# One prompt tile's gate matrix by scattered adds in DRAM, and row gathers paced anew

## The chip, the cores and the metric

One core of a Trainium2 chip runs the whole program. The metric is device time in microseconds (us) from the start to the end of an execution of the program; the profiled execution has its own time, given below beside the runs'. The engines are called as in the profile: PE (TensorE, matrix products), DVE (VectorE), ACT (ScalarE), POOL (GpSimd) and SP (SyncE, which only issues DMAs here). Each takes its instructions in a fixed order that was set when the program was built. DMAs are issued by SP, ACT and POOL.

## What is computed

An encoder layer is applied to two batches with shared weights: a prompt of 512 tokens and a sample of 256, of 1024 features. After attention and an output projection comes PEER, a layer of 128 x 128 = 16384 single-neuron experts:

```
q   = (xc @ w_q)                                  # 8 heads, two halves of 128
sc  = einsum('cpzk,znk->cpzn', q, sub_keys)       # scores of 128 keys for each half
top_v, top_i = top_k(sc, 16)
cand = top_v[:, :, 0, :, None] + top_v[:, :, 1, None, :]
best, pos = top_k(cand, 16)                       # 16 experts for each head and token
eidx = take_along_axis(cand_idx, pos)             # i * 128 + j
g   = softmax(best)
act = gelu(einsum('cd,cpkd->cpk', xc, u[eidx]))
out = einsum('cpk,cpkd->cd', g * act, v[eidx])    # 8 x 16 = 128 experts for each token
```

So each token weighs 128 of 16384 experts. All is in float32, and large products are made of three products of split halves.

## The kernel before

The tokens are six tiles of 128: four of the prompt (t = 0 to 3) and two of the sample (4, 5). The two parts of PEER go different ways.

**The sample tiles by gathers.** For each token the 128 rows of `uv` (u and v side by side, 8 KB a row) are fetched by indirect DMAs from POOL (line 738): one DMA fetches the c-th expert's row for all 128 tokens, so there are 256 of them, used in 128 pairs. DVE makes the dot product with u (740), ACT the gelu, and DVE adds weight x v to `acc` (748). There are four `row` buffers. A list `early` (725 to 728) says behind which DVE instruction the first dot product of each pair may stand at the earliest: 24 pairs stand in the routing, and 104 behind the low-half splits `low_of[j]` of the blocks j = 36 to 255, evenly. These are order marks without a semaphore.

**The prompt tiles densely.** For all 128 x 128 experts the hidden values of 512 tokens are computed in 128 unit blocks (`hidden`, 601 to 609): a block loads 512 KB of u, splits it in high and low (`split`, 71 to 73; the low half on DVE from block 20 on), makes 24 products of 512 columns, and writes the gelu to DRAM as `h_d`. In the value blocks (693 to 715) two blocks at a time are read back (`gw`), multiplied by the gate matrix on DVE (701), split, and multiplied with v: 24 products a block again. Blocks 128 to 255 of `low_of` are the values.

**The gate matrix** says for each token how much each expert counts: mostly zeros. It is built tile by tile (643 to 670), beside unit blocks. `route_pairs` (442) finds the gates and one-hot sums of the indices; `picked` (622) turns them by 32 small products and a transpose. Then for each group of 8 tokens DVE builds one `oij` (655) and three `og` (659), PE makes 24 small bf16 products (666), and ACT copies two banks (669). After 32 tokens ACT writes a 2 MB block to `g_d` (670). A tile has 16 groups; four tiles have 64. The values read `g_d` back in 16 loads of 2 MB (`gates`, 683).

Unit blocks 0 to 15 run beside the prompt's key routing (612); the others follow the gate build in the program (671), and the scheduler mixes both.

The first stages: the sample's projection, then the sample's attention mixed with the prompt's projection `in_project` (353), whose weights SP loads in pieces of 256 KB into three buffers (140), one for every 12 products.

Of the kernel before, what the change touches and what calls it, by code (L numbers as in the profile page):

```python
# [11 lines left out]
F32 = mybir.dt.float32  # L12
# [4 lines left out]
OP = mybir.AluOpType  # L17
AX = mybir.AxisListType
# [3 lines left out]
P = 128  # L22
D = 1024
# [7 lines left out]
NK = 128  # L31
# [13 lines left out]
NCAND = 64  # L45
FIRST_GATHER = 36
FILL = 16
NOSYNC = mybir.DependencyInfo(mybir.DependencyClass.NoSync, mybir.DependencyReason.DATA)


@with_exitstack
def tile_kernel(ctx, tc, xs_in, relb, onehot, logm, g1, w_in, gqk, lamv, gdiff, w_out, g2,
# [46 lines left out]
    x1_d = [dram.tile([P, D], F32, name=f"x1_d{t}") for t in range(NT)]  # L99
    g_d = dram.tile([DENSE * P // TB, P, NK, TB], F32, name="g_d")  # L100

# [8 lines left out]
    def stage():  # L110
        return late.tile([P, D], F32, tag="st4", name="st4", bufs=3)
# [38 lines left out]
    def in_project(lhs, n, pj, hrs, banks, lows=None):  # L150
# [12 lines left out]
        project(lhs, n, w_in, 6, banks, evac, lows)  # L163

    def attention(n, pj, hrs, mix, order, psc, ptr):
        w = n * P
# [22 lines left out]
        def probs(pl, q, toe):  # L189
            qh, kh, kl = pl  # L190
            ps = bank(psc[next(turn) % len(psc)], "psc")
            T.matmul(ps[:, :w], qh[:, q * P:(q + 1) * P], kh[:, :w], start=True, stop=False)
            T.matmul(ps[:, :w], qh[:, q * P:(q + 1) * P], kl[:, :w], start=False, stop=True)
            sc = att.tile([P, 512], F32, name="sc", bufs=4)
            mx = const.tile([P, 1], F32, name="mx", bufs=6)
            V.tensor_tensor_reduce(sc[:, :w], ps[:, :w], toe[:, 512 + P * q - w:512 + P * q][:, ::-1], -1.0, 3.0e38,
                                   OP.add, OP.min, mx)
            sm = const.tile([P, 1], F32, name="sm", bufs=6)
            S.activation(sc[:, :w], sc[:, :w], AF.Exp, bias=mx, scale=-1.0, accum_out=sm)
            rc = const.tile([P, 1], F32, name="rc", bufs=6)  # L200
            V.reciprocal(rc, sm)
            return sc, rc
# [146 lines left out]
    mixS = [stage().rearrange("p (d c) -> p d c", d=4) for _ in range(2)]  # L349
    attention(2, pjS, hrS, mixS, ORDER, [ps_sc], [ps_tr])  # L350
    pjP = [ppP.tile([P, 4, 2, 512], F32, tag="pj", name=f"pjP{k}") for k in range(3)]
    hrP = const.tile([P, 4, 2, 2, 8], F32, name="hrP")
# [289 lines left out]

    nxt = picked(0)
    for t in range(DENSE):
        ijT, gp_ = nxt
        if t + 1 < DENSE:
            nxt = picked(t + 1)
        for tb in range(P // TB):
            gb = gm.tile([P, NK, TB], F32, name="gb")
            for tq in range(TB // TQ):  # L650
# [11 lines left out]
                for c4 in range(TQ // 4):  # L662
# [6 lines left out]
                    S.copy(gb[:, :, o:o + 4].rearrange("p j t -> p t j"), pg)  # L669
            nc.scalar.dma_start(g_d[t * (P // TB) + tb], gb)  # L670
    for j in range(FILL, NK):
        hidden(j, G if j < 20 else V)
    left.close()
    rqx.close()
# [8 lines left out]
    def gates(jb):  # L683
        gblk = dp.tile([P, DENSE * P // TB, JB, TB], F32, name="gblk")
        nc.sync.dma_start(gblk, g_d[:, :, jb * JB:(jb + 1) * JB, :].rearrange("b i j t -> i b j t"))
        return gblk

# [5 lines left out]
    for jp in range(NK // 2):  # L693
        jj = 2 * jp % JB
        wh, wl = (late.tile([P, 2, 2, 512], F32R, tag=f"x{i}", name=f"w{i}") for i in range(2)) if jp == 0 else (wh, wl)
        if jj == 0:
            gblk = gates(2 * jp // JB)
        ge = dp.tile([P, 2, 512], F32, name="gw", bufs=3)
        nc.sync.dma_start(ge, h_d[jp])
        ge4 = ge.rearrange("p k (b t) -> p k b t", t=TB)  # L700
        V.tensor_tensor(ge4, ge4, gblk[:, :, jj:jj + 2].rearrange("p b k t -> p k b t"), op=OP.mult)
        gh, gl = wh[:, jp % 2], wl[:, jp % 2]
# [22 lines left out]
    early = marks[32:48] + marks[51::4][:8]  # L725
    rest = 128 - len(early)
    span = 2 * NK - FIRST_GATHER
    early += [low_of[FIRST_GATHER + k * span // rest] for k in range(rest)]
    for t in (4, 5):
# [76 lines left out]
```

## Time and profile before

| | |
|---|---|
| three runs | 2286.49, 2292.71, 2293.56 us; median 2292.71 |
| the profiled execution | 2291.37 us, its span 2289.4 us |
| mean granted TensorE clock | 0.976 of full speed |
| busy: PE, DVE, ACT, POOL | 94%, 79%, 40%, 37% of the span |
| moved by DMA | 617.65 MB, 270 GB/s on the mean |

The span runs from the first to the last instruction. Stages on its axis: up to about 430 us projections and attention, up to 590 the sample's output projection and routing, up to 790 the prompt's output projection and key routing with unit blocks 0 to 15, from 855 to 1345 the gate build beside unit blocks, to 1550 unit blocks alone, then the values to the end. Busy time is an average over such stages; which engine or transfer sets the time has to be read in each.

### The profile page before, as it was taken

To read this page: it belongs to the slowest core of one execution; us is meant where nothing else is said; L and a number is where in the kernel's file an instruction comes from. 1 tells how busy PE (TensorE), PEld (TensorE's weight loads), DVE (VectorE), ACT (ScalarE), POOL (GpSimd) and SP (SyncE) were. 2 spreads that over 40 slices of the span, in tenths; PEclk is the share of its full clock that TensorE was granted. 3 is DMA by queue.
4 is the path that set the end of the run, shared out by engine and by line. 5 is a ranking of instruction groups with operands and counts; after the bars stand their busy time and mean duration, and the time that the engine had idled before them with its cause. 6 is when DMAs were issued, how large, how long until landed. Compare 5 with 4: busy or idle time off the path is not lost.

```text
span 2289.4 us, 31065 instructions
## 1 busy us (share of the span) xinstructions
PE 2156.3 (94%) x11312; PEld 1774.7 (78%) x11312; DVE 1799.5 (79%) x3500; ACT 915.5 (40%) x1476; POOL 858.4 (37%) x626
## 2 busy tenths in 40 slices
PE   6999999957999989999999988999999999999998
PEld 4788789846787777878888876887788778888786
DVE  4645379996688999989999965666788878887786
ACT  4665587622332234545555532322233223323232
POOL 4767776623465632222423322221222322222221
PEclk9999999969999999999999998999999999999999
DMA  5534333314477776789899899897999999999985
GB/s 183 174 114 128 99 123 97 106 37 155 168 280 246 271 273 224 284 302 346 320 349 350 333 386 340 336 352 285 354 354 369 349 334 365 398 376 329 374 341 187
DMA packets 198553, 617.65 MB, mean 270 GB/s; under 512 B 15888, under 2 KB 82064, under 8 KB 163584
## 3 DMA queue, kind: packets, MB, share of 16 engines
q1 hardware_dynamic: 139840, 278.70, 35.1%
q0 software_dynamic: 36864, 268.45, 31.0%
q10 hardware_dynamic: 21696, 68.53, 7.8%
q8 instruction: 88, 1.44, 0.3%
q14 instruction: 65, 0.53, 0.1%
HBM read 542.17 MB, written 73.45 MB: 269 GB/s over the span
## 4 chain that ended last, share of the span: by engine, by line
PE 39%; issue 32%; DVE 11%; POOL 11%; DMA 5%; ACT 1%; SPq 0%; POOLq 0%; ACTq 0%; DVEq 0%
POOL row L738 9%; PE pu L69 5%; PE pu L67 5%; PE pu L68 5%; PE pacc L68 3%; PE pacc L69 3%; PE pacc L67 3%; DMA row<-in_uv_dram,eidx 3%; PE py L67 2%; PE py L68 2%; PE py L69 2%; PE pg L666 2%; PE pq L69 2%; PE pq L67 1%; PE pq L68 1%
## 5 line engine op out<-in xcount | busy, mean ns | idle before, releaser
L738 POOL DMA_INDIRECT row<-in_uv_dram,eidx x256 | 424.7, 1659 | 1147.8 <-DVE acc L748 1004.4
L72 ACT CAST hi<-raw 128x1024 fp32r<-128x1024 f32 x276 | 289.5, 1052 | 628.4 <-PE pu L68 223.7
L67 PE MATMUL pu<-x2p,hi 128*128 128x512 f32 x1024 | 408.4, 399 | 15.6 <-ACT hi L72 15.5
L69 PE MATMUL pu<-x2p,lo 128*128 128x512 f32 x1024 | 408.4, 399 | 12.7 <-DVE lo L73 10.6
L67 PE MATMUL py<-w,hi 128*128 128x512 f32 x1024 | 401.5, 394 | 16.0 <-ACT hi L72 13.6
L73 DVE TENSOR_TENSOR lo<-raw,hi 128x1024 fp32r<-128x1024 f32 x238 | 290.1, 1221 | 155.5 <-ACT hi L72 126.4
L68 PE MATMUL pu<-x2p,hi 128*128 128x512 f32 x1024 | 405.9, 396 | 0.0
L68 PE MATMUL py<-w,hi 128*128 128x512 f32 x1024 | 401.0, 392 | 0.0
L740 DVE CUSTOM_DVE_ANT_0 row<-row,st 128x1024 f32<-128x1024 f32 x256 | 330.2, 1295 | 62.0 <-DMA row<-in_uv_dram,eidx 61.8
L748 DVE SCALAR_TENSOR_TENSOR acc<-row,wgt,acc 128x1024 f32<-128x1024 f32 x256 | 328.9, 1285 | 5.5
L69 PE MATMUL py<-w,lo 128*128 128x512 f32 x1024 | 301.3, 390 | 2.8 <-DVE lo L73 2.8
L67 PEld LDWEIGHTS py<-w,hi 128*128 128x128 f32 x1024 | 193.6, 189 | 64.4 <-ACT hi L72 21.7
L67 PEld LDWEIGHTS pu<-x2p,hi 128*128 128x128 f32 x1024 | 195.0, 190 | 58.1 <-ACT hi L72 16.3
L69 PEld LDWEIGHTS pu<-x2p,lo 128*128 128x128 f32 x1024 | 194.5, 190 | 56.6 <-DVE lo L73 14.6
L69 PEld LDWEIGHTS py<-w,lo 128*128 128x128 f32 x1024 | 192.4, 188 | 43.5 <-DVE lo L73 3.7
L68 PEld LDWEIGHTS py<-w,hi 128*128 128x128 f32 x1024 | 193.8, 189 | 40.3 <-DVE w L73 0.3
L68 PEld LDWEIGHTS pu<-x2p,hi 128*128 128x128 f32 x1024 | 194.8, 190 | 38.6
L669 ACT COPY gb<-pg 128x512 f32<-128x512 f32 x128 | 132.6, 1145 | 78.5 <-PE pg L666 77.5
L73 POOL TENSOR_TENSOR wl<-wraw,wh 128x512 fp32r<-128x512 f32 x88 | 116.4, 1329 | 59.7 <-ACT wh L72 59.0
L72 ACT CAST w<-gw 128x1024 fp32r<-128x1024 f32 x64 | 67.1, 1050 | 151.7 <-PE py L69 151.0
L666 PE MATMUL pg<-og,oij 128*128 128x128 bf16 x1536 | 108.9, 220 | 4.2 <-DVE og L659 4.2
L745 ACT ACTIVATE wgt<-h 128x2 f32<-128x2 f32 x128 | 26.1, 204 | 212.0 <-DVE h L740 211.0
(309 smaller groups left out, 3666.7 us busy)
## 6 DMA issues: line engine op xcount, KB each, us to landing
raw<-in_uT_dram SPq DMA_DIRECT2D x128, 512.0 KB, 5.9
raw<-in_uv_dram SPq DMA_DIRECT2D x128, 512.0 KB, 7.9
h_d<-ge ACTq DMA_DIRECT2D x128, 256.0 KB, 5.6
g_d<-gb ACTq DMA_DIRECT2D x16, 2048.0 KB, 8.7
gblk<-g_d SPq DMA_DIRECT2D x16, 2048.0 KB, 17.2
gw<-h_d SPq DMA_DIRECT2D x64, 512.0 KB, 7.5
wraw<-in_w_in_dram SPq DMA_DIRECT2D x96, 256.0 KB, 2.8
toe<-bias_d SPq DMA_DIRECT2D x24, 448.0 KB, 4.2
```

The costliest lines, as they stand in the source:

```text
L67: T.matmul(ps, ah, bh, start=start, stop=False)
L68: T.matmul(ps, ah, bl, start=False, stop=False)
L69: T.matmul(ps, al, bh, start=False, stop=stop)
L72: S.copy(hi, raw)
L73: return (low or G).tensor_tensor(lo, raw, f(hi), op=OP.subtract)
L666: T.matmul(pg[:, c], oij[:, 0, c4 * 4 + c], og[k][:, c4 * 4 + c], start=k == 0, stop=k == 2)
L669: S.copy(gb[:, :, o:o + 4].rearrange("p j t -> p t j"), pg)
L738: G.indirect_dma_start(out=r, out_offset=None, in_=uv, in_offset=bass.IndirectOffsetOnAxis(ap=eidx[t][:, b + k:b + k + 1], axis=0))
L740: dot = V.tensor_tensor_reduce(r[:, :D], r[:, :D], x2r[t], 1.0, 0.0, OP.mult, OP.add, h[:, k:k + 1])
L745: S.activation(wgt, h, AF.Gelu)
L748: V.scalar_tensor_tensor(acc, rows[k][:, D:], wgt[:, k:k + 1], acc, op0=OP.mult, op1=OP.add)
```

## The change

For prompt tile 0 the gate matrix is no longer built by PE. A DRAM tile `s_d` of 128 x 128 x 128 floats (8 MB) is filled with zeros by eight writes from SP in the sample attention. After `route_pairs` of tile 0, DVE computes for each token and each of its 128 experts the address (i x 128 + j) x 128 + token. Then 128 indirect DMAs from POOL each add one gate for each of the 128 tokens into `s_d`. All are writes to one DRAM tile, so the program makes each wait for the one before. Their order marks are the splits of blocks 22 to 117, 0.75 block apart. `g_d` holds three tiles. The values load 512 KB of `s_d` and 1.5 MB of `g_d` for each 8 blocks, and the multiplication by gates becomes two instructions.

The order marks of the 104 later pairs change: 66 stand behind blocks 30 to 127, 38 behind 128 to 251.

```diff
-FIRST_GATHER = 36
 FILL = 16
+SCAT = 1
+FIRST_SCATTER = 22
+LAST_SCATTER = 118
+PACE = ((66, 30, 128), (38, 128, 252))
...
-    g_d = dram.tile([DENSE * P // TB, P, NK, TB], F32, name="g_d")
+    g_d = dram.tile([(DENSE - SCAT) * P // TB, P, NK, TB], F32, name="g_d")
+    s_d = [dram.tile([P, NK, P], F32, name=f"s_d{t}") for t in range(SCAT)]
...
-            V.reciprocal(rc, sm)
+            sums.append(V.reciprocal(rc, sm))
...
     attention(2, pjS, hrS, mixS, ORDER, [ps_sc], [ps_tr])
+    zero = stage()
+    tc.add_manual_dep(V.memset(zero, 0.0).ins, sums[8].ins.name, NOSYNC, reason="order")
+    for s_ in s_d:
+        for h in range(8):
+            nc.sync.dma_start(s_.rearrange("i j t -> i (j t)")[:, h * 2048:(h + 1) * 2048]
+                              .rearrange("i (a n) -> i a n", n=D), zero[:, None].to_broadcast([P, 2, D]))
...
-    nxt = picked(0)
-    for t in range(DENSE):
+    tok = gm.tile([P, 1], F32, name="tok", bufs=1)
+    G.iota(tok, pattern=[[0, 1]], base=0, channel_multiplier=1, allow_small_or_imprecise_dtypes=True)
+    scat = []
+    for t in range(SCAT):
+        gt, si = (o[t][:, 0].rearrange("p k h -> p (k h)") for o in (tv, ti))
+        ei, ej = route_pairs(rq, t, gt)
+        for m in (8, 4, 2):
+            V.tensor_tensor(ej[:, :m], ej[:, :m], ej[:, m:2 * m], op=OP.add)
+        i_, j_ = (rq.tile([P, NPK], F32, name="n1_") for _ in range(2))
+        V.tensor_reduce(i_, ei.rearrange("p m r -> p r m"), axis=AX.X, op=OP.add)
+        V.tensor_tensor(j_, ej[:, 0], ej[:, 1], op=OP.add)
+        V.scalar_tensor_tensor(i_, i_, float(NK), j_, op0=OP.mult, op1=OP.add)
+        V.tensor_scalar(i_, i_, float(P), tok, op0=OP.mult, op1=OP.add)
+        V.tensor_copy(si, i_)
+        scat.append((si, gt))
+    nxt = picked(SCAT)
+    for t in range(SCAT, DENSE):
...
+    for k in range(NPK * SCAT):
+        t, c = k % SCAT, k // SCAT
+        si, gt = scat[t]
+        put = G.indirect_dma_start(out=s_d[t].rearrange("i j (t one) -> (i j t) one", one=1),
+                                   out_offset=bass.IndirectOffsetOnAxis(ap=si[:, c:c + 1], axis=0),
+                                   in_=gt[:, c:c + 1], in_offset=None, compute_op=OP.add)
+        after = low_of[FIRST_SCATTER + k * (LAST_SCATTER - FIRST_SCATTER) // (NPK * SCAT)]
+        tc.add_manual_dep(put.ins, after.ins.name, NOSYNC, reason="order")
...
-        gblk = dp.tile([P, DENSE * P // TB, JB, TB], F32, name="gblk")
+        gs = dp.tile([P, SCAT, JB, P], F32, name="gs")
+        for t in range(SCAT):
+            nc.sync.dma_start(gs[:, t], s_d[t][:, jb * JB:(jb + 1) * JB])
+        gblk = dp.tile([P, (DENSE - SCAT) * P // TB, JB, TB], F32, name="gblk")
...
-        ge4 = ge.rearrange("p k (b t) -> p k b t", t=TB)
-        V.tensor_tensor(ge4, ge4, gblk[:, :, jj:jj + 2].rearrange("p b k t -> p k b t"), op=OP.mult)
+        for ge4, g4 in ((ge[:, :, :SCAT * P].rearrange("p k (b t) -> p k b t", t=P), gs),
+                        (ge[:, :, SCAT * P:].rearrange("p k (b t) -> p k b t", t=TB), gblk)):
+            V.tensor_tensor(ge4, ge4, g4[:, :, jj:jj + 2].rearrange("p b k t -> p k b t"), op=OP.mult)
...
-    rest = 128 - len(early)
-    span = 2 * NK - FIRST_GATHER
-    early += [low_of[FIRST_GATHER + k * span // rest] for k in range(rest)]
+    for n, j0, j1 in PACE:
+        early += [low_of[j0 + k * (j1 - j0) // n] for k in range(n)]
```

## Rows read from the trace of the kernel before

**Rows 1.** The page: busy time and share; bandwidth in 40 equal slices.
```profile
PE 2156.3 (94%) x11312; PEld 1774.7 (78%) x11312; DVE 1799.5 (79%) x3500; ACT 915.5 (40%) x1476; POOL 858.4 (37%) x626
...
GB/s 183 174 114 128 99 123 97 106 37 155 168 280 246 271 273 224 284 302 346 320 349 350 333 386 340 336 352 285 354 354 369 349 334 365 398 376 329 374 341 187
```

**Rows 2.** Windows of three stages: us, busy us of each engine, clock, DMA share, GB/s.
```profile
855.00:1345.00 490.00, 480.04 (x3273) 390.20 (x3272) 463.32 (x739) 247.61 (x319) 139.90 (x71) 0.99 0.86 316
1345.00:1560.00 215.00, 195.77 (x833) 159.20 (x832) 131.13 (x156) 57.84 (x86) 49.66 (x34) 0.95 0.91 344
1560.00:2280.00 720.00, 703.56 (x3097) 576.59 (x3096) 576.60 (x660) 203.56 (x249) 181.88 (x114) 1.00 0.91 344
```

**Rows 3.** Timeline of PE in three short windows: start, us, what, count.
```profile
920.03 2.63 PE L666 MATMUL pg<-og,oij 128*128 128x128 bf16 x44
...
1005.65 1.06 PE L628 MATMUL pt<-identb,ej 128*128 128x128 bf16 x16
...
1480.01 0.39 PE L69 MATMUL pu<-x2p,lo 128*128 128x512 f32 x1
...
1481.83 0.39 PE L68 MATMUL pu<-x2p,hi 128*128 128x512 f32 x1
```

**Rows 4.** Windows, instructions on the tile `pu` alone: PE, PEld, ACT, then as above.
```profile
855.00:1345.00 490.00, 406.50 (x1638) 303.77 (x1637) 40.54 (x68) 0.99 0.86 316
1345.00:1550.00 205.00, 185.15 (x793) 150.69 (x791) 20.10 (x34) 0.96 0.92 350
```

**Rows 5.** Groups by shape, 855 to 1560 us: busy us, mean ns, idle before.
```profile
L748 DVE SCALAR_TENSOR_TENSOR acc<-row,wgt,acc 128x1024 f32<-128x1024 f32 x100 | 127.9, 1279 | 1.3
...
L740 DVE CUSTOM_DVE_ANT_0 row<-row,st 128x1024 f32<-128x1024 f32 x100 | 121.7, 1221 | 31.8 <-DMA row<-in_uv_dram,eidx 31.8
...
L655 DVE TENSOR_TENSOR oij<-ijT,iotaj 128x2048 bf16<-128x2048 bf16 x64 | 77.5, 1216 | 0.4 <-PE pg L666 0.4
...
L659 DVE TENSOR_TENSOR og<-oij,gp__9507 128x1024 bf16<-128x1024 bf16 x48 | 30.2, 683 | 0.0
```

**Rows 6.** Lines of the sample's index arithmetic: ns min/median/max, first and last start.
```profile
L523 DVE TENSOR_REDUCE ijf<-ei x2: 3571/3690/3809, 493.0 to 519.0; 128x128 f32<-128x2048 bf16 x2
...
L528 DVE CAST eidx<-ijf x2: 2090/2134/2178, 506.9 to 540.5; 128x128 uint32<-128x128 f32 x2
```

**Rows 7.** POOL's gathers: two issues, each one's landing, then 900 to 1320 us.
```profile
1448.97 1.86 POOL L738 DMA_INDIRECT row<-in_uv_dram,eidx  x1 [9.27 <-DVE acc L748]
1451.13 0.94 POOL L738 DMA_INDIRECT row<-in_uv_dram,eidx  x1 [0.30 <-issue]
...
DMA to landing us min/median/max: 7.5/7.5/7.5
...
DMA to landing us min/median/max: 9.0/9.0/9.0
...
L738 POOL DMA_INDIRECT row<-in_uv_dram,eidx x58: 936/1678/5755, 905.5 to 1318.3; - x58
...
DMA to landing us min/median/max: 5.4/10.2/14.1
```

**Rows 8.** Timeline of DVE: the dot product after the next one.
```profile
1462.04 1.23 DVE L740 CUSTOM_DVE_ANT_0 row<-row,st 128x1024 f32<-128x1024 f32 x1
```

**Rows 9.** The page's DMA issues: count, KB each, median us from issue to landing.
```profile
g_d<-gb ACTq DMA_DIRECT2D x16, 2048.0 KB, 8.7
...
out_dram<-yo SPq DMA_DIRECT2D x8, 256.0 KB, 2.0
```

**Rows 10.** SP's issues near 115 us (timeline), and the projection's weight loads.
```profile
113.01 4.05 SPq L140 DMA_DIRECT2D wraw<-in_w_in_dram  x3
...
126.99 0.33 SPq L140 DMA_DIRECT2D wraw<-in_w_in_dram  x1
...
DMA to landing us min/median/max: 2.5/2.8/4.5
```

## The prediction before the run

> **What bounds the kernel now.** I read the page first, then the windows by stage, then single lines. TensorE (PE) is busy for 94% of the span [rows 1], so the question is whether it is really full. [rows 3] show eight steps of the unit products between 1480.01 and 1481.83 us: 1.82 / 8 = 0.2275 us each, so a block of 24 takes 24 x 0.2275 = 5.46 us at best. [rows 4] count 1638 such products in 855 to 1345 us (68 blocks beside the gate build; call it stage A, 7.2 us a block) and 793 in 1345 to 1550 us (33 blocks; stage B, 6.2 us a block). The values, 1560 to 2280 us (stage C), are at 704 of 720 us. The gate build's bf16 products come at (2.63 - 0.22) / 43 = 0.056 us each [rows 3], with one product's 0.22 us taken off. PE's need in A is then 68.25 x 5.46 + 1536 x 0.056 = 373 + 86 = 459, with some 6 for the picked tiles 465 of 490; in B 180 of 205; in C 128 blocks, less the two that ran in B, are 690, and 64 small products for `x1` (about 7, an estimate: a quarter of the columns, at twice the time per column) make 697 of 720. So PE sets the time nearly everywhere, with roughly 25 us of gaps in each of the three stages.
>
> [rows 2] show the runners-up. In A, VectorE (DVE) is busy for 463 of 490 us: it is full there too. In B it falls to 131 of 215, but the DMA share is 0.91 at 344 GB/s. In C, DVE is at 577 of 720, DMA 0.91. The best of the 40 slices moved 398 GB/s [rows 1]; I take that as the ceiling that this kernel has shown. GpSimd (POOL) is busy for 140 of 490 us in A.
>
> **Gate build, one tile of four taken out.** PE loses 384 x 0.056 = 21.5 us and the 32 products and one transpose of `picked` (1.06 us for 16 [rows 3], so about 1.9 for 32): 23.4 us, all on the path, since PE is the bound. DVE loses 16 groups of one `oij` and three `og`: 16 x (1.216 + 3 x 0.683) = 52 us [rows 5]. The 32 ACT copies and 8.4 MB of `g_d` writes go too; neither sets the end.
>
> **Index arithmetic, added.** `route_pairs` stays. The sample's rows price the rest: the reduction 3.69 and the integer copy 2.13 us [rows 6]; with adds of about the same shapes I take 10 us of DVE. It lies in front of the first gate build, beside unit products: nothing on the path as long as PE has blocks ready, at most 10.
>
> **Zeroing, added.** Eight writes of 1 MB go into SP's queue in the sample attention, in front of the weight loads of the prompt projection, which PE is living on there. Bounds: 8.4 MB at 398 GB/s is 21 us; at the pace of a 2 MB `g_d` write (8.7 us [rows 9]) it is 35. A weight load now lands in 2.5 to 4.5 us [rows 10]; one issued behind the whole burst would land 21 to 35 us late. But SP issued its loads of 113.01 us and then nothing of this kind until 126.99 [rows 10], so some 10 us pass without a need, and three buffers of 12 products (2.7 us each) cover another 8. PE could stand still between 0 and about 17 us; I take 5, nearer to the covered end, because the ordering of those loads can move around the burst.
>
> **Row gathers moved.** Before, 24 pairs sit on marks in the routing and 104 are spread evenly over blocks 36 to 256; so (128 - 36) x 104 / 220 = 43 lie beside the units. Now it is 66: 23 pairs more beside the units, 23 fewer beside the values. A pair costs DVE 2 x 1.22 + 2 x 1.28 + 0.3 = 5.3 us [rows 5]: 122 us move. Beside the units DVE then has 463 + 131 - 52 + 10 + 122 = 674 us of work in 705 - 23 = 682: full. DMA has 316 x 0.490 + 344 x 0.215 = 228.8 MB there, plus 46 gathers of 1.05 MB = 48.2, less 8.4: 268.6 MB in 682 us = 394 GB/s, at the ceiling of 398. The marks are only lower bounds in the order ("not before"), so I expect some pairs to slip into the values, which have room: DVE 577 - 122 = 455 of 720, DMA (247.7 - 48.2) / 720 = 277 GB/s. For this stage I book +2 us of crowding. The values hold about 23 us of PE gaps; of these I take 6 back, since waits for rows there are a small part; 0 and 20 are the ends.
>
> **The extra multiply and the 16 `gs` loads.** `gw` x gates is one instruction of 1.22 us now and two of the same total columns then; the split costs perhaps 0.1 us x 64, in a stage where DVE becomes two thirds busy: nothing, and at most 6 if pairs slip into it heavily. The gate bytes loaded are the same.
>
> **The 128 scatters ("puts").** No accumulating DMA is in the trace. On POOL, a gather occupies 2.17 us from issue to next issue (1448.97 to 1451.13 [rows 7]), and a put also makes 128 entries: 128 x 2.17 = 278 us. POOL then has 140 + 50 + 278 + 46 x 1.86 = 554 of 682 us: it fits. The landing matters more, since all puts add into one tile in DRAM and the program orders them: each waits on POOL until the one before has landed, and every gather behind it on POOL waits too; DVE's dot products wait for those, and behind them, in the same queue, the `lo` splits that PE needs. A gather with nothing ahead landed 7.5 us after issue, the next, issued 2.16 later, 9.0 after its own, so 11.2 after the first: each gather in line adds 3.7 us [rows 7]. A put moves almost no data, so alone I estimate 7.5 - 3.7 = 3.8 us (a 256 KB plain write lands in 2.0 [rows 9]; a gather in 7.5: the two bounds). Behind two gathers it is about 11.5 after the first gather's issue. A period of two gathers and two puts then takes, in the order gather, put, gather, put: the first put lands at 7.8, the second is issued, the next gather 2.2 later: 10.0 us. In the order gather, gather, put, put: 11.5 + 2.2 = 13.7 us. Room: 96 blocks for 128 puts are 68 blocks of A (490 us) and 28 of B (174) less 23 = 641 us, 10.0 us per two puts. So the better order just fits, the worse doesn't. I book 0: rows are asked for early (the gather of 1448.97 fills the buffer that DVE reads at 1462.04, 13 us later [rows 7, 8], and lands after 7.5), which takes up single waits, and pairs that slip out of this stretch shorten the period.
>
> The Trainium skill ("DMA: Bandwidth & Descriptors", Rules for kernel authors) says that another access of the same bytes must wait for an accumulating DMA's semaphore; no run here shows it. The same page ("Anatomy of one DMA") has some 2.0 us fixed per DMA from POOL: by that estimate the chain alone would be 256 us and would fit.
>
> **Sum.** Against the profiled 2291.4 us (span 2289.4): - 23.4 + 5 + 2 - 6 = 2269. The median of the runs is 1.3 above the profiled one, so the sum stands for both within their spread.
>
> **Rivals.** *First, the put chain sets the pace* (slower): beside blocks 22 to 118, POOL stands in front of a put whose predecessor lies behind two gathers. It decides once two puts and two gathers take over 10.0 us. Price 0 to 3.7 x 64 = 237 us; at the mean of both orders, 1.85 x 64 = 118: 2269 + 118 = 2387. For it: the arithmetic of landings, and a gather median landing of 10.2 us in A [rows 7]. Against: the 13 us of lead, and POOL idle for 350 of 490 us in A. *Second, the units stage hits the DMA and DVE ceiling* (no change): 268.6 MB at 380 GB/s, between B's mean and the best slice, take 707 us, as long as before's 705; the gate saving is eaten there: 2291.4 + 5 - 8 = 2288. For it: both engines come out at 99%. Against: pairs may slip. *Third, the change doesn't do what it says*: DVE being full, the pairs slip back to where they were and the values gain nothing: 2269 + 6 = 2275. *Fourth, the zeroing burst* takes its full 17: 2269 + 12 = 2281.
>
> **How the numbers follow.** Forecast 0.38; first rival 0.35; second 0.16; third 0.07; fourth 0.04. A measurement of this kernel can tell about 0.3% from no change (2284.5 to 2298). Faster: 0.38 + 0.07 + 0.02 = 0.47; within: 0.16 + 0.02 of the fourth with its neighbours = 0.18; slower 0.35. The lower end is the sum with all of C's gaps back and no cost for zeroing: 2291.4 - 23.4 - 20 = 2248. The upper end takes in the first rival at its mean price, with a little above: 2400; beyond it lies that rival's worse order, about 0.12. The likeliest case alone: 2250 to 2284.
>
> **What would show it.** Right: the gate products fall to 1152, A shortens to about 52 blocks at the same 7.2 us, B's blocks stay near 6.2, C's fall from 5.7 to about 5.6; puts come at 5 us intervals without idle time in front of them. First rival: POOL's idle time is named by the landing of `s_d`, DVE waits for `row` far above the 31.8 us of A and B now [rows 5], and unit blocks go above 7 us after the gate build is done. Second: DMA share at 1.0 through the units and ACT waiting for `raw`. Zeroing: a PE gap near 115 to 135 us with ACT waiting for `wraw`. The forecast is wrong if a put alone takes clearly more than 5 us: then even the better order doesn't fit.

## The result: slower by 11.7%, and one standstill holds most of it

The changed kernel takes 2561.3 us (median of 4 runs, 2551.74 to 2568.39) against 2293.14 us before: ratio 1.117, 95% interval 1.1122 to 1.1218. The forecast was 2269, in a range of 2248 to 2400. The profiled execution of after has a span of 2563.4 us, 274 over that of before.

A change spread over several stages is best dated by instructions that both kernels have: the GELUs of the unit blocks (`ge`) and the first and last product of the values (`py`). All are starts in us, from the timelines. The third column is an experiment that is told below, the changed kernel with its puts left out.

| | before | after | after without the puts |
|---|---|---|---|
| GELU of block 16 | 792 | 804 | 800 |
| GELU of block 88 | 1304 | 1345 | 1297 |
| GELU of block 127, the last | 1548 | 1557 | 1528 |
| first product of the values | 1549 | 1808 | 1530 |
| last product of the values | 2280 | 2554 | 2252 |

From mark to mark, after against before: + 12 up to block 16; 541 for 512 up to block 88, + 29; 212 for 244 up to block 127, - 32; 251 for 1 until the values start, + 250; 746 for 731 in the values, + 15. The sum is 274. So the unit blocks as a whole lost nothing against before (against the third column, which is what they could have been, they lost 24), and nearly everything lies between the last unit block and the first product of the values.

The page of after shows the same at a glance: PE's busy time is within 2 us of before's [rows 1], in a span 274 us longer, and one of the 40 slices moved nothing at all.

```profile
PE 2155.0 (84%) x10895; PEld 1770.2 (69%) x10895; DVE 1763.8 (69%) x3507; ACT 885.3 (35%) x1440; POOL 1061.8 (41%) x755
...
GB/s 181 167 113 230 112 118 81 62 125 191 263 250 274 257 153 230 320 341 299 337 361 354 342 347 325 295 229 0 266 313 306 263 311 271 300 294 266 303 281 107
```

The windows of its stages, with columns as in [rows 2], then those of the tile `pu` alone, as in [rows 4]:

```profile
859.00:1345.00 486.00, 445.18 (x2788) 357.94 (x2787) 407.29 (x684) 211.02 (x276) 239.63 (x133) 0.96 0.83 288
1345.00:1557.00 212.00, 211.71 (x935) 174.96 (x933) 145.15 (x179) 65.88 (x99) 96.13 (x59) 1.00 0.97 346
1557.00:1815.00 258.00, 7.08 (x20) 5.67 (x21) 117.89 (x161) 7.85 (x26) 138.66 (x90) 0.51 0.65 215
1816.00:2554.00 738.00, 714.37 (x3113) 582.03 (x3112) 473.71 (x569) 199.21 (x227) 110.44 (x70) 0.99 0.77 273
```

```profile
859.00:1345.00 486.00, 385.36 (x1537) 288.78 (x1536) 38.53 (x65) 0.96 0.83 288
1345.00:1557.00 212.00, 211.71 (x935) 174.96 (x933) 23.14 (x40) 1.00 0.97 346
```

In the first stage PE is idle for 41 of 486 us (10 of 490 before); in the second it is full, at full clock, with the puts running beside it; in the third nothing runs on it until 1807.9 us: the 20 matmul records there are the first products of the values. From the last GELU to the first product it was 1.6 us before and is 251.2 now. The waits of PE's weight loads (engine, line, releaser: us in all, times, longest) name that stretch, and the waits of SP's queue from 1500 to 1850 us name what is behind it:

```profile
PEld py L70 <- ACT w L75: 251.6, 1, 251.6
PEld pu L72 <- DVE lo L76: 32.8, 16, 7.4
```

```profile
SPq L721 <- DMA s_d<-tv,ti: 233.3, 1, 233.3
```

L721 is the load of `gs` from `s_d`. It can't be issued until the last put has landed (at 1794.2 us), and without `gs` there are no gated hidden units, no `w`, no product. The timelines of POOL and of SP show the last puts and the load right behind them:

```profile
1788.08 1.56 POOL L703 DMA_INDIRECT s_d<-tv,ti  x1 [1.64 <-DMA s_d<-tv,ti]
1791.32 1.55 POOL L703 DMA_INDIRECT s_d<-tv,ti  x1 [1.69 <-DMA s_d<-tv,ti]
```

```profile
1550.56 10.40 SPq L600 DMA_DIRECT2D raw<-in_uv_dram  x3
1794.29 0.33 SPq L721 DMA_DIRECT2D gs<-s_d  x1
```

The 128 puts run from 888 to 1791 us, 7.1 us each on average, where the marks left room for 5. Why they are so slow beside the units shows on POOL from 1440 us on:

```profile
1440.06 1.71 POOL L776 DMA_INDIRECT row<-in_uv_dram,eidx  x1 [4.96 <-DVE acc L786]
1442.39 1.68 POOL L776 DMA_INDIRECT row<-in_uv_dram,eidx  x1 [0.62 <-DVE acc L786]
1444.37 1.61 POOL L703 DMA_INDIRECT s_d<-tv,ti  x1 [0.30 <-issue]
1450.94 1.71 POOL L776 DMA_INDIRECT row<-in_uv_dram,eidx  x1 [4.96 <-DVE acc L786]
```

The order on POOL, fixed when the kernel is built, has come down to gather, gather, put, at one pair in 10.9 us: one put to 10.9 us here. In 54 of the 127 intervals between puts two gathers stand (median 8.8 us), in 25 one (6.3). At the end 25 puts are left over and follow each other alone. The landings of puts (the time from a DMA's issue to the arrival of its data) from 1720 to 1795 us, where hardly anything else moves, and from 1440 to 1470 us, behind two gathers each:

```profile
DMA to landing us min/median/max: 2.9/3.0/3.8
```

```profile
DMA to landing us min/median/max: 8.5/8.9/9.1
```

### The profile page after: what moved, and what is told of

It reads as the page before. It is cut to its first block, busy times and chain, and to the rows that moved or that the text cites. A ratio compares the mean times of both kernels' runs of the same rounds, so it can differ in the third digit from the quotient of the medians.

```text
span 2563.4 us, 30359 instructions
## 1 busy us (share of the span) xinstructions
PE 2155.0 (84%) x10895; PEld 1770.2 (69%) x10895; DVE 1763.8 (69%) x3507; ACT 885.3 (35%) x1440; POOL 1061.8 (41%) x755
## 4 chain that ended last, share of the span: by engine, by line
PE 40%; issue 25%; DMA 13%; DVE 12%; POOL 8%; ACT 1%; SPq 0%; POOLq 0%; ACTq 0%; DVEq 0%
PE pu L72 6%; PE pu L70 6%; PE pu L71 6%; DMA row<-in_uv_dram,eidx 5%; DMA s_d<-tv,ti 5%; POOL row L776 5%; PE pacc L70 3%; PE pacc L71 3%; PE pacc L72 3%; POOL s_d L703 2%; DMA gw<-h_d 2%; PE pq L72 2%; PE pg L693 1%; DVE row L778 1%; DVE acc L786 1%
## 5 line engine op out<-in xcount | busy, mean ns | idle before, releaser
L776 POOL DMA_INDIRECT row<-in_uv_dram,eidx x256 | 379.7, 1483 | 932.9 <-DVE acc L786 832.7
L70 PE MATMUL py<-w,hi 128*128 128x512 f32 x1024 | 403.0, 396 | 256.5 <-ACT w L75 251.2
L70 PEld LDWEIGHTS py<-w,hi 128*128 128x128 f32 x1024 | 194.8, 190 | 302.7 <-ACT w L75 251.6
L703 POOL DMA_INDIRECT s_d<-tv,ti x128 | 254.5, 1988 | 240.0 <-DMA s_d<-tv,ti 226.6
L72 PE MATMUL py<-w,lo 128*128 128x512 f32 x1024 | 316.3, 395 | 18.3 <-DVE lo L76 18.0
L72 PEld LDWEIGHTS pu<-x2p,lo 128*128 128x128 f32 x1024 | 194.9, 190 | 75.3 <-DVE lo L76 32.8
L740 DVE TENSOR_TENSOR gw<-gw,gs 128x256 f32<-128x256 f32 x64 | 27.0, 422 | 239.9 <-DMA gw<-h_d 239.9
L696 ACT COPY gb<-pg 128x512 f32<-128x512 f32 x96 | 99.5, 1136 | 74.0 <-PE pg L693 72.9
```

Of the source, the lines that this page charges most:

```text
L70: T.matmul(ps, ah, bh, start=start, stop=False)
L72: T.matmul(ps, al, bh, start=False, stop=stop)
L703: put = G.indirect_dma_start(out=s_d[t].rearrange("i j (t one) -> (i j t) one", one=1), out_offset=bass.IndirectOffsetOnAxis(ap=si[:, c:c ...
L740: V.tensor_tensor(ge4, ge4, g4[:, :, jj:jj + 2].rearrange("p b k t -> p k b t"), op=OP.mult)
L776: G.indirect_dma_start(out=r, out_offset=None, in_=uv, in_offset=bass.IndirectOffsetOnAxis(ap=eidx[t][:, b + k:b + k + 1], axis=0))
```

## The experiments

All are edits of the changed kernel unless something else is said; line numbers in rows are those of the kernel shown. "Standstill" is PE's one wait at the first product of the values; "units end" is the GELU of block 127.

| kernel | median us | ratio to before (95%) | last put | units end | standstill |
|---|---|---|---|---|---|
| changed kernel | 2561.3 | 1.117 (1.112 to 1.122) | 1791 | 1557 | 251.6 |
| e1 values read another array | 2525.6 | 1.103 (1.100 to 1.107) | 1801 | 1548 | 160.8 |
| e2 no puts | 2261.4 | 0.987 (0.984 to 0.990) | none | 1528 | none |
| e3 pace of before | 2463.3 | 1.075 (1.071 to 1.079) | 1716 | 1558 | 174.8 |
| e4 before, and zeroing | 2295.5 | 1.001 (0.999 to 1.004) | none | 1563 | none |
| e5 two accumulators | 2397.8 | 1.043 (1.040 to 1.047) | 1618 | 1603 | 48.2 |
| e6 few gathers beside units | 2498.5 | 1.088 (1.085 to 1.091) | 1567 | 1640 | none |
| e7 as e1, indices kept | 2334.1 | 1.017 (1.014 to 1.021) | 2168 | 1589 | none |
| e8 indices kept | 2581.0 | 1.123 (1.119 to 1.127) | 1824 | 1600 | 232.4 |
| e9 bursts of 4 | 2658.7 | 1.160 (1.153 to 1.166) | 1876 | 1602 | 299.7 |
| e10 bursts of 8 | 2698.9 | 1.175 (1.168 to 1.181) | 1936 | 1622 | 339.9 |
| e11 no gathers beside units | 2557.4 | 1.117 (1.114 to 1.120) | 1522 | 1590 | none |
| e12 two accumulators, zeros spread | 2361.0 | 1.029 (1.025 to 1.034) | 1577 | 1573 | 38.4 |

**Are the puts the whole loss?** e2 leaves the puts out (the gates of prompt tile 0 stay zero), with all the rest of the change; e4 adds the zeroing alone to the kernel before.

```diff
-    for k in range(NPK * SCAT):
+    for k in range(0):
```

> Leaves out the 128 puts: tile 0's gate matrix stays zero; the zeroing, the index arithmetic, the loads of s_d and the new pace of the gathers stay. It measures the change's gain without its cost. Theory (the puts are the whole loss, and the sum without them was right): 2269, at most 2280. Rival (DMA and DVE ceiling beside the units): 2288. Rival (the new pace of the gathers is the loss): above 2400.

```diff
 (e4, to the kernel before)
+    s_d = [dram.tile([P, NK, P], F32, name="s_d0")]
...
+    zero = stage()
+    tc.add_manual_dep(V.memset(zero, 0.0).ins, sums[8].ins.name, NOSYNC, reason="order")
+    for s_ in s_d:
+        for h in range(8):
+            nc.sync.dma_start(s_.rearrange("i j t -> i (j t)")[:, h * 2048:(h + 1) * 2048]
+                              .rearrange("i (a n) -> i a n", n=D), zero[:, None].to_broadcast([P, 2, D]))
```

> The kernel before with nothing added but the zeroing: memset and eight 1 MB writes into a DRAM tile that nobody reads, at the same place. Theory of the sum: + 5 us, 2298. Rival (burst in front of the projection's weight loads): + 17, 2310. Rival (hidden): + 0 to 2, 2293 to 2295.

They are. e2 takes 2261.4 us, 0.987 of before (0.984 to 0.990), and e4 is within half a per cent of before. Everything in the change but the puts brings 29 us; the puts cost 300. By the marks of the profiled executions 250 of these lie in the standstill, 24 in the unit blocks and 24 in the values. The three stages of e2, columns as in [rows 2]:

```profile
859.00:1297.00 438.00, 428.26 (x2765) 345.53 (x2764) 402.06 (x677) 210.04 (x274) 117.01 (x69) 0.99 0.87 323
1297.00:1528.00 231.00, 220.24 (x936) 179.19 (x936) 159.70 (x199) 65.98 (x100) 75.20 (x44) 0.96 0.96 360
1535.00:2252.00 717.00, 705.29 (x3114) 580.55 (x3112) 567.51 (x705) 201.36 (x246) 166.90 (x110) 1.00 0.90 338
```

**What holds the values?** In e1 the values read an array that is ready long before (tile 0's gates are left out), so no data ties them to the last put. In e8 the puts' indices and gates are copied to a tile that lives to the end, so that their space needn't be free before the values' buffers open; e7 is both (its tile 0 gates are left out too).

```diff
 (e1, e7)
-            nc.sync.dma_start(gs[:, t], s_d[t][:, jb * JB:(jb + 1) * JB])
+            nc.sync.dma_start(gs[:, t].rearrange("p j t -> p (j t)"), h_d[jb].rearrange("p k t -> p (k t)"))
 (e7, e8)
-        scat.append((si, gt))
+        keep = stage()
+        si_, gt_ = keep[:, :NPK].bitcast(U32), keep[:, NPK:2 * NPK]
+        V.tensor_copy(si_, si)
+        V.tensor_copy(gt_, gt)
+        scat.append((si_, gt_))
```

> Leaves out tile 0's gates: the values read another DRAM tensor of the same shape where they read s_d, so nothing waits for the puts; everything else of the change stays, the 128 puts too. Theory (end of the chain): the 252 us for which PE stands still between the units and the values are the wait for the last put; without that wait the time is 2561 - 252 = about 2310 us (2295 to 2330), with no single wait of PE above 20 us. Rival (rate): the puts take the gathers' place on POOL wherever they run, so the loss moves into DVE's waits for rows beside the values, and the time stays above 2400.

> As the kernel whose values read another array in place of the added-up matrix (tile 0's gates are left out), and besides the indices and gates of the puts lie in a tile that lives to the end, so that the values' pool doesn't wait for the last put to read them. Theory (the values were held by two ties, the data of the matrix and the space of the puts' indices; with both gone the puts may drag on beside the values): the first gates multiply runs within 40 us of the last unit block, the puts still end near 1750 us or later, the standstill is under 60 us; some of the gain is lost later if VectorE's order still puts products of rows that wait for puts ahead of value blocks: 2300 to 2400 us. Rival (the order of work on VectorE holds the values whatever they read): as the kernel with one tie gone, 2500 to 2540.

> The changed kernel with only the indices and gates of the puts moved to a tile that lives to the end; the values still read the added-up matrix. Theory (either tie alone holds the values): as the changed kernel within 40 us, 2520 to 2600 us, standstill of TensorE 210 to 260 us. Rival (the space was the whole tie, and the read of the matrix is met by an earlier end of the puts): under 2400 us.

e1 missed by 215 us. The time is that of its rival, but most of the loss is still one standstill and not waits beside the values. Its loads of `gs` were issued at 1552 us, yet PE stood still for 160.8 us:

```profile
PEld py L70 <- ACT w L75: 160.8, 1, 160.8
```

On VectorE 43 dot products of rows stand in a line behind the last split that runs beside the units and before the first gates multiply, at 1706 us, and those rows are gathered behind puts; the order of the instructions is the same as in the changed kernel. With the second tie gone as well (e7) the standstill is gone, and with the second alone (e8) it is 232.4 us:

```profile
PEld py L70 <- ACT w L75: 232.4, 1, 232.4
```

That the second tie works through the order shows on VectorE: with the indices kept, its first gates multiply starts at 1370 us (e7) and 1377 us (e8), beside the units, and with the indices in their old place at 1706 (e1) and 1805 (changed kernel). So there are two ties, and either one is enough: the data of `s_d`, and the space of the puts' indices, which lie in buffers that are closed before those of the values open, so that the work of the values is placed behind the puts. e8 is 20 us over the changed kernel: its other order on the engines ends the unit blocks 43 us later, and its standstill is 19 shorter; why the units end later was not followed up. e7, whose puts drag on beside the values to 2168 us, is still 1.7% slower than before (1.4 to 2.1).

**What sets the pace of the puts?** e3, e6 and e11 change only where the gathers stand.

```diff
 (e3)
-PACE = ((66, 30, 128), (38, 128, 252))
+PACE = ((104, 36, 256),)
 (e6)
+PACE = ((16, 30, 128), (88, 128, 256))
 (e11)
+PACE = ((104, 128, 256),)
```

> The change with the gathers' even pace of before (104 pairs over blocks 36 to 255). In the changed kernel's trace a put follows the one before after 3.2 us at best with no gather between, 6.3 in the median with one, 8.8 with two; so fewer gathers between the puts shorten the chain. Theory (chain, lengthened by gathers in line): some 40 pairs instead of 60 stand beside the puts, 40 x 8.8 + 88 x 4.5 = 750 us instead of 906, the last put about 1640, PE's wait about 85 us, the time about 2390 (2340 to 2440). Rival (the puts alone are too slow): no change from 2561. Rival (new pace is the loss): about 2293.

> 16 pairs of gathers beside the units in place of 66, 112 beside the values. Theory (it is the gathers between two puts that make the chain long): with few gathers in the queue most puts follow each other in 3 to 4 us, the last lands before 1550 us, and TensorE doesn't stand still at the first gates multiply; what is then late is the end, since 112 pairs at 10 to 11 us each need some 1150 us beside the values: 2550 to 2750 us for another reason. Rival (the puts are slow by themselves, or tied to the units' weights): the last put still lands after 1700 us and the standstill stays over 150 us.

> None of the 104 paced pairs stands beside the units, all beside the values; the puts are alone on POOL's queue from 888 us on. Theory (what a put costs is its own chain, about 5 us beside the units' loads and 3.2 us only where nothing else moves, and each gather before it adds about 2.8 us; the unit blocks lose only where VectorE waits for rows that lie behind puts): 128 x 4.9 = 627 us, so the last put lands at 1490 to 1540 us, the unit blocks end as without puts, 1520 to 1550 us, and TensorE doesn't stand still; the time is then set by 104 pairs after 1530 us at 8.3 us each, 2400 to 2520 us. Rival (the puts themselves slow the units, by their traffic or the waits on POOL): unit blocks end after 1590 us though no row is waited for.

Fewer gathers, faster puts: the last one is issued at 1791, 1716, 1567 and 1522 us with 66, 43, 16 and none of the pairs marked for the units. What is marked is not what runs, though: from 855 us to the last GELU the four kernels issue 102, 100, 45 and 13 gathers. So e3 says nothing of the units. There it has as many gathers as the changed kernel and the same 82 puts, and its units end at the same time; its gain lies behind them, where the last 46 puts stand with 2 gathers in place of 44. It missed its 2340 to 2440 us by 23. e6 and e11 do thin the gathers out.

e11 gives the price of the chain alone. Its 57 puts from 1100 to 1400 us, and PE in the same stretch (first line of its windows; columns as above):

```profile
L703 POOL DMA_INDIRECT s_d<-tv,ti x57: 1552/1552/2482, 1103.3 to 1398.5; - x57
...
DMA to landing us min/median/max: 3.0/5.1/9.6
```

```profile
1060.00:1360.00 300.00, 300.00 (x1822) 249.58 (x1819) 141.71 (x159) 129.66 (x154) 100.02 (x57) 1.00 0.62 181
```

Two things follow. With no gather in the chain, 56 steps from put to put take 295.2 us, 5.3 us each. All 128 puts at that pace are 670 us, while blocks 22 to 118 last 641 us by the prediction's own count: there is no room for a single gather. (Over the whole chain the mean is (1522 - 886) / 127 = 5.0, because from 1464 us on, when hardly any loads run (22 GB/s from 1455 to 1520 us), the puts follow each other every 3.2 us.) And PE is busy for 300 of 300 us at full clock, so in this stretch a put by itself takes nothing from the unit blocks.

A closer look at e11 shows what goes with the 5.3 us. From 1330 to 1462 us it issues 24 puts and 24 loads of `uT`, one of each in every 5.44 us, the time of a block. In the 8 places where both landings are on record, the put lands 0.2 to 0.4 us before a load that was issued 1.3 to 1.5 us after it. In these places a put landed only when a load of 512 KB was all but through. Beside the gate build the two are less in step, and whether the load holds the put no run shows.

The second half of e11 is the miss: units end at 1590, not 1520 to 1550, though rows were waited for only 8.9 us. That is where its rival put them, but not for the rival's reason. SP's queue shows why, by its timeline and its longest wait for a landing:

```profile
1432.69 27.53 SPq L600 DMA_DIRECT2D raw<-in_uT_dram  x6
1525.35 0.33 SPq L721 DMA_DIRECT2D gs<-s_d  x1
...
1537.71 0.33 SPq L600 DMA_DIRECT2D raw<-in_uT_dram  x1
```

```profile
SPq L721 <- DMA s_d<-tv,ti: 65.1, 1, 65.1
```

The load of `gs` stands in SP's order ahead of the last blocks' weights (`uT`); it waits 65.1 us for the last put, they wait behind it, and PE stands still 63.5 us among the unit blocks. 1590 - 63 = 1527, where the units of e2 end. The time of e11, over the expected 2400 to 2520, is set by the gathers, which go on when the last product is done (2300 us). In e6 the same wait on SP is 25.6 us. The rest of what its unit blocks lose is the first rival of the prediction: waits of PE for `lo` of 74.3 us in 19 (32.8 in 16 in the changed kernel), behind rows that stand behind puts. e6 missed the expected 1550 for its last put by 17 us and the expected 2550 to 2750 by 52; its last product starts at 2359 us, and the gathers set its end too. A wait of PE costs more than it lasts, as its timeline behind one of 4.37 us shows:

```profile
1503.27 0.79 PE L72 MATMUL pu<-x2p,lo 128*128 128x512 f32 x1 [4.37 <-DVE lo L76]
1503.87 0.63 PE L70 MATMUL pu<-x2p,hi 128*128 128x512 f32 x1
1504.29 0.63 PE L71 MATMUL pu<-x2p,hi 128*128 128x512 f32 x1
...
1509.66 0.40 PE L72 MATMUL pu<-x2p,lo 128*128 128x512 f32 x1
1509.90 0.39 PE L70 MATMUL pu<-x2p,hi 128*128 128x512 f32 x1
```

The products then come every 0.42 us (1503.87 to 1504.29) for 6 us, with a granted clock of 0.50 from 1503.3 to 1509.3 us, the lower of the two levels (1.2 GHz), before 0.24 is back.

**Can the order on POOL save it?** e9 sets the order by hand, four puts in a row and then the four gathers of two pairs; e10 does so with eight and eight.

```diff
-PACE = ((66, 30, 128), (38, 128, 252))
+PACE = ((64, 24, 120), (40, 128, 252))
+BURST = 4
...
+        if k % BURST == 0:
+            tc.add_manual_dep(put.ins, after.ins.name, NOSYNC, reason="order")
+        elif k:
+            tc.add_manual_dep(put.ins, puts[-1].ins.name, NOSYNC, reason="order")
+        puts.append(put)
...
+                if 0 <= u < 64:
+                    m = BURST * (u * 2 // BURST)
+                    tc.add_manual_dep(got.ins, puts[m + BURST - 1].ins.name, NOSYNC, reason="order")
+                    if m + BURST < 128 and True and u % (BURST // 2) == BURST // 2 - 1 and k == 1:
+                        tc.add_manual_dep(puts[m + BURST].ins, got.ins.name, NOSYNC, reason="order")
```

> The order on POOL is set by hand: four puts in a row, then the four gathers of two pairs, 32 times over (64 pairs beside the units, 40 beside the values). Theory (a put costs 3.2 us behind a put and 8.5 to 9 behind gathers, and one put to a pair of gathers was the loss): 32 x (3 x 3.2 + 8.8) = 589 us, so that the last put lands 1480 to 1600 us, the standstill of TensorE at the first gates multiply falls under 50 us, and the time is 2280 to 2400 us; what stays over the kernel without puts (2261 us) is lost in the unit blocks. Rival (the puts hold the units instead, since VectorE waits for rows that lie behind four puts): the standstill goes, but the unit blocks end after 1640 us and the time is 2400 us or more.

> As the bursts of four, with eight puts and then the eight gathers of four pairs. Theory: 16 x (7 x 3.2 + 8.8) = 499 us for the puts, so the last lands no later than with bursts of four and the time is within 30 us of it or better. Rival (rows behind a burst of 26 to 31 us hold VectorE and with it the splits): VectorE waits for rows in the unit blocks over 150 us (37.9 us in six waits between 895 and 1020 us in the changed kernel), the units end 40 us or more later than with bursts of four, and the time is over it by as much.

Both theories missed: the last put came at 1876 and 1936 us, the standstill grew, and e10 is 40 us over e9. POOL of e9:

```profile
1410.48 0.97 POOL L782 DMA_INDIRECT row<-in_uv_dram,eidx  x1 [0.30 <-issue]
1411.76 0.94 POOL L782 DMA_INDIRECT row<-in_uv_dram,eidx  x1 [0.30 <-issue]
1413.00 0.94 POOL L782 DMA_INDIRECT row<-in_uv_dram,eidx  x1 [0.31 <-issue]
1414.24 1.61 POOL L705 DMA_INDIRECT s_d<-tv,ti  x1 [0.30 <-issue]
1428.44 1.81 POOL L705 DMA_INDIRECT s_d<-tv,ti  x1 [12.58 <-DMA s_d<-tv,ti]
1434.03 1.56 POOL L705 DMA_INDIRECT s_d<-tv,ti  x1 [3.78 <-DMA s_d<-tv,ti]
```

The put behind four gathers took 14.2 us to the next issue, the next one 5.6, not 3.2. The 3.2 that the expectation was worked out with came from a stretch in which PE stood still and hardly anything else moved: the price of a put was carried to a place with other traffic. And while a burst is waited for, no gather is issued. A group of four and four takes (1836 - 1002) / 28 = 29.8 us, by the starts of the ninth and the 121st put.

**Is it the chain?** e5 lets the puts turn about between two zeroed arrays, so that a put waits for the one before the last; the values load and add both. e12 is the same with the second array's zeros written in eight pieces along the prompt attention.

```diff
 (e5, e12)
...
-        put = G.indirect_dma_start(out=s_d[t].rearrange("i j (t one) -> (i j t) one", one=1),
+        put = G.indirect_dma_start(out=s_d[k % 2].rearrange("i j (t one) -> (i j t) one", one=1),
...
+            gn = [gs] + [dp.tile([P, SCAT, JB, P], F32, name=f"gs{m}") for m in range(1, 2)]
+            for m in range(2):
+                nc.sync.dma_start(gn[m][:, t], s_d[m][:, jb * JB:(jb + 1) * JB])
+            for m in range(1, 2):
+                V.tensor_tensor(gs, gs, gn[m], op=OP.add)
 (e12)
+    n0 = len(sums)
...
+    for s_ in s_d[1:]:
+        for h in range(8):
+            zd = nc.sync.dma_start(s_.rearrange("i j t -> i (j t)")[:, h * 2048:(h + 1) * 2048]
+                              .rearrange("i (a n) -> i a n", n=D), zero[:, None].to_broadcast([P, 2, D]))
+            tc.add_manual_dep(zd.ins, sums[n0 + 1 + h * (len(sums) - n0 - 2) // 8].ins.name, NOSYNC, reason="order")
```

> The puts turn about between two zeroed matrices, so that a put waits for the one before the last; the values load both and add them on VectorE (8 MB more are zeroed and 8 MB more loaded). Theory (each put waits for the landing of the one before it, 3 us alone and 8.5 to 9 behind two gathers, and the order built round that length puts one put to a pair of gathers; 128 of them end at 1800 us, after the unit blocks): with half the waits the last put lands before 1600 us, the standstill of TensorE at the first gates multiply (251.6 us in the changed kernel) falls under 30 us, and the time is 2265 to 2320 us. Rival (the price of a put is its issue on POOL or its traffic, not the chain): the last put stays near 1800 us, the standstill over 200 us, the time 2540 to 2600.

> As the kernel with two accumulators, with the second one's 8 MB of zeros written in eight pieces along the prompt attention (500 to 600 us, where the DMA engines were busy 20% to 46%) in place of one burst of 16 MB beside the first one. Theory (the second burst cost 36 us at the first unit block, the rest of the loss is in the unit blocks, the standstill of 48 us and the values): the first unit block is back at 602 to 610 us, the time 2345 to 2375 us, still slower than before. Rival (a write of 8 MB costs the same 30 us wherever it stands): 2385 to 2405 us.

Half the waits take 164 us off the time with the marks of the pairs as they were, and the standstill falls from 251.6 to 48.2 us in e5 and 38.4 in e12:

```profile
PEld py L70 <- ACT w L75: 48.2, 1, 48.2
...
PEld py L70 <- ACT w L75: 38.4, 1, 38.4
```

So the chain is the cause, not POOL's issues or the traffic, of which e5 has more. It acts in two ways that these runs don't separate: by the waits themselves, and by the order that was built round them (125 of the 128 puts of e5 are issued before the last GELU, 82 in the changed kernel). e5 missed its 2265 to 2320: the second burst of zeros moved block 16 from 804 to 838 us, the puts began 34 us later, and the standstill didn't fall under 30. In e12, 37 us better than e5 and inside its expected 2345 to 2375, block 16 is at 813. No version that computes all gates is faster than before. e12 is over e2 by 13 us at block 16, 32 in the unit blocks, 36 up to the first product of the values and 19 from there to the end, 100 in all, of which the 29 that the rest of the change brings pay a third.

## Why the prediction was wrong, step by step

**The step that failed** is the one on the 128 puts, "I book 0": the better order "just fits" 10.0 us for two puts and two gathers. Three parts of it were measured:

- *The price of a put.* I put 3.8 us for one alone. It lands in 3.0 us where nothing else moves, but in 5.1 beside the units' weight loads with no gather in line, and one follows the other after 5.3 (e11): 10.6 for two puts without any gather, where there was room for 10.0. With one gather between puts they came at a median of 6.26 us, so 12.5 for two puts and two gathers in the better order, not 10.0. The worse order was priced at 13.7; e9's bursts, another form of it, took 29.8 / 2 = 14.9. Neither fits. The test that the prediction set itself, "wrong if a put alone takes clearly more than 5 us", came out just past its mark: at 5.3 nothing is left for gathers.
- *Which order it would be.* I thought the order free to be gather, put, gather, put. It was fixed at build, and from 1440 us on it is gather, gather, put, with one put to 10.9 us. There POOL's idle time is `row` waiting for `acc` (107.4 us from 1320 to 1556), and only 12.4 the landing of `s_d`; from 890 to 1320 us the landing leads, 161.9 us. Pairs did slip out of this stretch, as the prediction hoped (51 ran beside the units, 66 were marked), and the period was still too long.
- *What stands behind the last put.* The prediction followed the wait along POOL and VectorE and never asked who reads `s_d`. The values do, all of them, from the first block on: a chain that runs over its time isn't spread over the units but is paid in full at one point. Of that overrun, (7.1 - 5.0) x 127 = 267 us, 250 are found there.

**The first rival** (slower, 2387, chance 0.35) named the cause and the sign, and its bound, 237 us on top, was not far under what the puts cost against e2, 300. Its place was wrong. What it describes, VectorE waiting for rows and PE for `lo`, is there, in the gate build: VectorE waits for rows 71.9 us in 25 from 859 to 1557 us, 10.1 in 10 in e2, and the stretch from block 16 to 88 takes 541 us against 498. But 19 come back up to block 127, and its sign, "unit blocks go above 7 us after the gate build is done", didn't come: 212 us for 39 blocks are 5.4. The range ended at 2400, just above this rival's mean price; the time lies beyond even its worse order (2506).

**The other terms came out near their size**, which e2 shows since it is the forecast without the puts: 2261.4 against 2269. For one of them that was luck.

- *Gate build*, - 23.4: from block 16 to 127 e2 takes 729 us, before 756, so - 27 with the crowding in it, which was booked at + 2.
- *Zeroing*, + 5: e4 puts it at 3 us (interval - 2 to 9). It was issued at 193 us, not near 115, and PE was busy for 54.9 of the 60 us from 180 on, 59.4 before: 4.4 us. In the traces the first GELU of a unit block is at 602 us in e4 and 595 before, one trace each. The place was wrong, the size about right.
- *Row gathers moved*: 23 pairs were to go from the values to the units. From 855 us to the last GELU e2 issues 106 gathers, before 98, and beside the values 110, before 116: three or four pairs moved. VectorE and the DMA engines never got the load that was worked out for the units, and in this the third rival was right.
- *Values*, - 6: 722 us in e2 against 731, but not for the reason given, since hardly a pair left them. In the changed kernel, where 23 pairs did leave (70 gathers beside the values, 44 in the standstill), they took 746. The right size is luck.
- *The second rival*, the DMA ceiling: the stage from 1345 us on ran at a DMA share of 0.97 with PE full, and the gate saving was not eaten in e2. There is no loss from it here, but as hardly any gathers moved, the load that it was worked out for never came.
- *The extra multiply*, "nothing": not seen in e2. In the changed kernel VectorE waited beside the values for loads of `gw` for 142.3 us in 36 (12.6 in 12 before), at a lower DMA share than before, 0.77. The late start isn't the reason: the values of e3 start at 1732 us and take 717, with 13.3 us of such waits. What goes with it is the number of gathers left: the changed kernel, e8, e9 and e10 have 70 to 84 beside the values, wait 90 to 145 us for `gw` and take 736 to 746; before, e2, e3 and e7 have 110 to 116, wait 10 to 18 and take 717 to 731. Why fewer gathers go with longer waits was not tried.

The Trainium skill ("DMA: Bandwidth & Descriptors", Rules for kernel authors) has another access of the same bytes wait for an accumulating DMA's semaphore; the trace agrees, POOL idles 226.6 us in 87 waits for `s_d`. By its 2.0 us fixed per DMA ("Anatomy of one DMA") the prediction estimated the chain at 256 us, which would fit. The measurement decides: the shortest interval between two puts of the changed kernel is 3.1 us, which makes 400, and 5.3 beside loads makes 670. The same page ("Latency and other measured facts") lets that fixed part grow with the load on memory; landings of 3.0 us without traffic and 5.1 at 181 GB/s agree with it in direction.

## What to carry to other kernels

Price a chain of dependent DMAs by its landing in the traffic that will stand beside it, multiply by its length, and compare that with the stretch it must fit before anything else is put into its queue. Then look at who reads its end: work that needs all of the chain pays the whole overrun at once, and so does everything behind that reader on its engine and queue. When a wait is cut and nothing moves, look for a second tie, of space or of order, before dropping the theory. And count what ran beside a stage before you book what a mark was to move there: of 23 pairs that were to change stages, e2 moved three or four.

## What the runs showed of the hardware that was not expected

- An accumulating DMA of 128 single floats lands in 3.0 us alone, in 5.1 beside some 180 GB/s of other loads (e11), in 8.9 behind two gathers of 1 MB on the same queue. In the last case (1440 to 1470 us) it lands 1.1 to 1.3 us after the second gather, though it touches other memory; in e11 it lands in step with a load from SP's queue that was issued after it (5.44 us a block).
- Eight writes of 1 MB cost 3 us in front of the prompt projection (e4); eight more right behind them moved block 16 by another 34 us (e5), 9 when they were spread over a later stage (e12).
- A wait of 4.4 us on PE was followed by 6 us at a granted clock of 0.50 (0.42 us a product, then 0.24; e6), so that this wait in the unit blocks cost more than it lasted.
